# A hybrid decoder block on one core: attention queries and keys turned by VectorE and DMA beside the delta rule, fewer short operations in threshold search and softmax, planner estimates by stage

## The chip, the core and the metric

The kernel runs on one core of a Trainium2 chip. TensorE (PE; PEld is its weight load) multiplies matrices into PSUM, VectorE (DVE), ScalarE (ACT) and GpSimd (POOL) work on SBUF and all but POOL on PSUM, and SyncE (SP) issues nearly all DMAs, one after the other in a fixed order. The metric is the device time of one execution in microseconds. Before the change it is 1774.93 us, the median of three runs from 1773.57 to 1776.5 us.

## The reference, cut to what matters

The input x has 1024 tokens of width 1024. One RMS-normed projection feeds two branches: a gated delta rule with 8 heads (chunked, with a triangular solve for each chunk and a state carried from chunk to chunk), and an attention in which an indexer picks 256 keys for each query. Their gated sum goes through an output projection and then a squared-ReLU MLP of width 4096. What the change touches is the attention branch:

```
a_q = rope(rms_norm(a_q))          # 1024 tokens, 8 heads of 128
a_k = rope(rms_norm(a_k))          # 1024 tokens, 2 heads of 128
score = sum_h w_idx * relu(q_idx . k_idx), causal
_, sel = lax.top_k(score, 256)     # for each query
s = (a_q . a_k[sel]) * 128**-0.5
p = softmax(s);  o = p @ a_v[sel]
```

## The kernel before, in words

All float32 products that matter are made of three single-pass matmuls: each operand is split into a rounded part and a remainder (names `hh` and `hl`, `kTh` and `kTl`, `qh` and `qlo`, ACT makes the first and DVE the second).

The work comes in stages that overlap. First, to about 250 us, the projections of the attention branch: queries and keys are normed, roped and written with tokens as rows to the DRAM tensors `QD` (1024 x 1024) and `KD` (1024 x 256). Then, to about 890 us, the delta rule: for each head PE projects its weights (`dd` matmuls, about 15 us for each group of 128 columns, whose raw weights `w` a DMA brings), and between them, in small float32 matmuls (`tt`, `jj`, `cc`, `oo`), it makes the chunk matrices, joins the inverse and scans the state. Each head's triangular solve runs on POOL, with DMAs ahead of it and behind it (`ZA`, `ZU`). Keys, values and outputs of a head are turned from rows to columns by DVE in 32 x 32 blocks and a DMA that puts the blocks in their places (`by_tokens`, L988, and `output`, L1302, by way of the DRAM tensors `TD` and `TO`).

Beside the delta rule runs the search of the indexer's threshold (`search`, L721): bit by bit from the 32nd down, it counts the scores that reach a candidate. One instance handles the query blocks 2 to 5 with four counts on DVE, one each handles the blocks 6 and 7 with a count on ACT (a sum of signs over 896 and 1024 columns). After each count it does three short DVE operations on one or four columns: `cand<-thr` sets the next bit, `tki<-cnt` judges the count, `thr<-thr,tki` keeps the bit. `select` (L784) then writes the masks.

The attention (about 895 to 1160 us) has 16 steps, one for each block of 128 queries and group of 4 heads (`ATT`). `loadq` (L1422) brings the 128 x 512 queries of a step from `QD` into `ql`. In `score` (L1479) PE turns them by four transposes (`s<-ident,ql`) into one of the two PSUM buffers `s`, ACT and DVE split that into `qh` and `qlo`, and PE multiplies with the keys, up to 512 keys at a time, into the same ring of two buffers. `kprep` (L1390) makes `kTh` and `kTl` in the same way ahead of the first step (`tt<-ident,w`, 16 transposes). `reduce` (L1516) takes each block of scores from PSUM: one DVE operation adds the mask, scales and takes the maximum; for the last block of a row a short one (`nm<-mx`) merges the maxima and changes the sign; ACT takes the exponential with that as bias, and DVE or ACT divides by the sum. `values_out` (L1545) turns the probabilities (`pt<-ident,pr`) and multiplies them with the values (`o`). The output projection (`dd<-hh,m`) fills in between. The MLP follows, to the end.

The order on each engine is fixed when the program is built: the class `Weave` (L2321) lets all these generators run against an estimate of time, takes the ready one of highest priority, and chains the instructions of each engine in that order. Its estimates are the constants of `call` (L2434 to L2459): for instance 0.417 ns for a column of a single-pass matmul, 0.07 us and one element in 1/960 us for DVE, at least 0.5 us for a DMA's issue, and 2.5 us (`SY_LATENCY`) until it has landed. Since every operation is recorded in `call`, all rows of the profile have its line, L2435, and are told apart by their tiles.

Of the kernel before, what the change touches and what calls it, by code (L numbers as in the profile page):

```python
# [20 lines left out]
P = 128  # L21
# [29 lines left out]
def body(tc, a, out, dbg=None):  # L51
# [98 lines left out]
    KD = dr.tile([S, 2 * P], F32, name="KD")  # L150
    GC = dr.tile([H, S], F32, name="GC")
# [467 lines left out]
    scores = {qb: mkp.tile([P, (qb + 1) * P], F32, name=f"sc{qb}") for qb in range(2, NB)}  # L619
# [101 lines left out]
    def search(cs, act):  # L721
        if act is None:
            V_.memset(cand, 0.0)
        yield ("scores", 5 if act is None else act)
        for bit in range(31, -1, -1):
            if bit < 31:
# [3 lines left out]
            if act is None:  # L730
# [5 lines left out]
                lim, cmp = float(TOPK), OP.is_ge  # L736
            else:
                yield "A"
                n = (act + 1) * P
                junk = scp.tile([P, S], F16, name="tkcm")  # L740
                A_.activation(junk[:, :n], scores[act], AF.Sign, scale=-1.0, bias=cand[:, cs],
                              accum_out=cnt[:, cs])
                lim, cmp = float(n - 2 * TOPK), OP.is_le
            yield
            if bit == 31:
                V_.tensor_scalar(thr[:, cs].bitcast(I32), cnt[:, cs], lim, -1.0, op0=cmp, op1=OP.add)
# [6 lines left out]
        if act is None:  # L753
            wv.done("search", 0)
            return


# [78 lines left out]
    for c in ((slice(0, 4), None), (slice(4, 5), 6), (slice(5, 6), 7)):  # L836
        wv.add(8, search(*c))
# [310 lines left out]

    def join(h):
# [203 lines left out]

    wv.add(1, gweights())
    wv.add(9, gdense())
    for u in (6, 5):
        wv.run(until=("put", u))
# [13 lines left out]
    wv.run(until=("masks",))  # L1371
    for c in "kv":
        wv.run(until=("turned", c, H - 1))
# [16 lines left out]
    def kprep():  # L1390
        yield ("out", H - 2)
        for half in range(2):
            t = slot(1, [P, 4, 256], F32)
            SY_.dma_start(t, KD.rearrange("(b p) c -> p b c", p=P)[:, half * 4:half * 4 + 4, :])
            hs = slice(half * HALF, (half + 1) * HALF)
            yield
            for g in range(2):
                yield tt.ready
                ps, slot_ = tt.get()
                for i in range(4):  # L1400
                    PE_.transpose(ps[:, i, :], t[:, i, g * P:(g + 1) * P], ident)
                yield
                pf = ps.rearrange("p a b -> p (a b)")
                A_.activation(kTh[g][:, hs], pf, AF.Copy)
                yield
                V_.tensor_tensor(kTl[g][:, hs], pf, kTh[g][:, hs].bitcast(F32), op=OP.subtract)
                tt.free(slot_)
# [14 lines left out]
    def loadq():  # L1422
        for idx, (qb, g) in enumerate(ATT):
# [3 lines left out]
            SY_.dma_start(ql, QD[qb * P:(qb + 1) * P, g * HALF:(g + 1) * HALF].rearrange("p (h d) -> p h d", h=4))  # L1427
# [51 lines left out]
    def score():  # L1479
        npr = 0  # L1480
        for idx, (qb, g) in enumerate(ATT):
            n = (qb + 1) * P
            yield ("ql", idx)
            yield ss.ready
            ps, slot_ = ss.get()
            ps = ps.rearrange("p (a b) -> p a b", a=4)
            for i in range(4):
                PE_.transpose(ps[:, i, :], lds["q", idx][:, i, :], ident)
# [1016 lines left out]
```

## Time and profile before

| | us |
|---|---|
| median of three runs | 1774.93 |
| the profiled execution | 1774.56 |
| its span, first to last instruction | 1772.8 |
| PE busy in the span | 1754.5 |
| DVE, ACT and POOL busy | 1306.0, 1017.4, 535.8 |

The profiled execution took 1.8 us more than its span (what lies around the program) and 0.4 us less than the median. [...] Matmuls are pipelined, so a row's duration (390 ns for 512 columns) is longer than the step from one start to the next (about 227 ns), and the price of an operation on PE is read from starts.

### The profile page before, as it was taken

How to read it: one execution, taken by the hardware profiler on the slowest of the kernel's cores; microseconds unless marked ns; L12 is line 12 of the kernel's file. 1: busy time of each engine (PE TensorE's matmuls, PEld its weight loads, DVE VectorE, ACT ScalarE, POOL GpSimd, SP SyncE). 2: the span in 40 equal slices, each digit the busy share in tenths (PEclk: the TensorE clock that was granted, in tenths of full speed). 3: DMA queues.
4: the chain of work that ended last, by engine and by line, in shares of the span. 5: the costliest groups of instructions: out<-in, count | busy, mean ns of one | idle time of the engine just before them, and what ended most of it. 6: DMA issues, size and time to landing. Idle time of an engine off the chain costs nothing.

```text
span 1772.8 us, 27516 instructions
## 1 busy us (share of the span) xinstructions
PE 1754.5 (99%) x9657; PEld 1466.5 (83%) x9657; DVE 1306.0 (74%) x2804; ACT 1017.4 (57%) x2074; POOL 535.8 (30%) x772
## 2 busy tenths in 40 slices
PE   9999999999999999999999999999999999999999
PEld 7987998888878888878877888888888888888887
DVE  6557759868788989896467776887666668969673
ACT  7555756666677564554456666676666663333331
POOL 0006430643362441734023121223233232222230
PEclk9999999999999999999999999999999999999999
DMA  5201244444455364445465221325544459373341
GB/s 166 84 13 48 72 129 108 96 121 108 103 134 110 78 144 105 104 110 124 136 222 161 74 81 54 119 84 173 172 161 137 158 198 369 118 251 118 95 138 52
DMA packets 316012, 222.86 MB, mean 126 GB/s; under 512 B 141193, under 2 KB 260194, under 8 KB 315874
## 3 DMA queue, kind: packets, MB, share of 16 engines
q1 hardware_dynamic: 315858, 221.10, 42.8%
q8 instruction: 76, 1.25, 0.3%
q14 instruction: 62, 0.51, 0.1%
q10 hardware_dynamic: 16, 0.00, 0.0%
HBM read 153.23 MB, written 67.83 MB: 125 GB/s over the span
## 4 chain that ended last, share of the span: by engine, by line
PE 89%; DVE 3%; DMA 3%; ACT 2%; SPq 1%; issue 1%; POOL 1%; POOLq 0%; ACTq 0%; DVEq 0%
PE dd L2435 52%; PE o L2435 16%; PE s L2435 7%; PE pt L2435 6%; PE cc L2435 2%; PE sq L2435 2%; PE tt L2435 2%; SPq L2435 1%; PE oo L2435 1%; PE jj L2435 1%; DMA vv<-TO 1%; DVE w L2435 1%; DMA m<-in_w_mlp_down_dram 0%; ACT pr L2435 0%; PE tp L2435 0%
## 5 line engine op out<-in xcount | busy, mean ns | idle before, releaser
L2435 PE MATMUL dd<-hh,w 128*128 128x512 f32 x1552 | 509.3, 401 | 0.0
L2435 PEld LDWEIGHTS dd<-hh,w 128*128 128x128 f32 x1552 | 286.2, 188 | 54.0 <-issue 2.1
L2435 PE MATMUL dd<-hl,w 128*128 128x512 f32 x776 | 310.8, 401 | 0.0
L2435 ACT ACTIVATE m<-m 128x512 fp32r<-128x512 f32 (+1 forms) x240 | 139.8, 625 | 79.1 <-PE o L2435 29.1
L2435 PE MATMUL dd<-hh,m 128*128 128x512 f32 x520 | 172.7, 396 | 0.9 <-ACT ph L2435 0.7
L2435 DVE TENSOR_TENSOR m<-m,m 128x512 fp32r<-128x512 f32 (+2 forms) x184 | 141.1, 794 | 38.7 <-ACT m L2435 33.5
L2435 PEld LDWEIGHTS dd<-hl,w 128*128 128x128 f32 x776 | 146.2, 188 | 26.5 <-issue 0.4
L2435 PE MATMUL dd<-w,hh 128*128 128x256 f32 (+1 forms) x704 | 164.7, 324 | 0.0
L2435 POOL TENSOR_TENSOR stmp<-sx,um 128x60 f32<-128x60 f32 (+24 forms) x186 | 86.4, 465 | 175.1 <-DMA um<-ZA 161.6
L2435 PEld LDWEIGHTS dd<-w,hh 128*128 128x128 f32 x704 | 118.0, 190 | 9.4 <-issue 0.5
L2435 PE MATMUL dd<-w,hl 128*128 128x256 f32 (+1 forms) x352 | 114.2, 324 | 0.0
L2435 PEld LDWEIGHTS dd<-hh,m 128*128 128x128 f32 x520 | 96.4, 188 | 19.2 <-ACT ph L2435 1.1
L2435 POOL TENSOR_TENSOR sx<-sx,stmp 128x60 f32<-128x60 f32 (+24 forms) x248 | 105.3, 425 | 19.4
L2435 DVE TENSOR_SCALAR_CACHE_REDUCE tkeq<-sc,cand 128x384 f16<-128x384 f32 (+3 forms) x128 | 103.0, 805 | 1.1
L2435 PE MATMUL dd<-hl,m 128*128 128x512 f32 x260 | 102.4, 394 | 0.0
L2435 POOL TENSOR_TENSOR m<-m,m 128x512 f32<-128x512 f32 x48 | 69.6, 1459 | 105.7 <-DVE m L2435 58.7
L2435 ACT ACTIVATE hh<-m 128x1024 fp32r<-128x1024 f32 x44 | 45.2, 1056 | 90.7 <-PE s L2435 42.0
L2435 ACT ACTIVATE ha<-m 128x1024 fp32r<-128x1024 f32 x44 | 45.3, 1056 | 86.0 <-PE o L2435 35.1
L2435 DVE TENSOR_TENSOR w<-w,w 128x1024 fp32r<-128x1024 f32 (+1 forms) x63 | 69.3, 1101 | 24.5 <-ACT w L2435 24.3
L2435 ACT ACTIVATE tkcm<-sc,cand 128x896 f16<-128x896 f32 x64 | 69.6, 1088 | 21.1 <-DVE cand L2435 18.8
L2435 PE MATMUL o<-hh,m 128*128 128x512 f32 x248 | 79.6, 389 | 0.0
L2435 PEld LDWEIGHTS dd<-w,hl 128*128 128x128 f32 x352 | 67.0, 190 | 4.5
(433 smaller groups left out, 4358.5 us busy)
## 6 DMA issues: line engine op xcount, KB each, us to landing
HD<-m SPq DMA_DIRECT2D x112, 256.0 KB
m<-HD SPq DMA_DIRECT2D x56, 512.0 KB
w<-in_w_in_dram SPq DMA_DIRECT2D x48, 512.0 KB
m<-in_w_mlp_up_dram SPq DMA_DIRECT2D x33, 512.0 KB
m<-in_w_mlp_down_dram SPq DMA_DIRECT2D x16, 512.0 KB
w<-in_x_dram SPq DMA_DIRECT2D x10, 512.0 KB
wraw<-in_w_in_dram SPq DMA_DIRECT2D x4, 1024.0 KB
es<-GC SPq DMA_DIRECT2D x8, 512.0 KB
```

What stands on the lines that cost most here:

```text
L2435: ins = f(*args, **kw)
```

## The change

1. A new generator `turn_attention` starts when the first head has been scanned. In 20 items (4 for the keys, 16 for the queries) it loads 256 KB from `KD` or `QD` into `ti`, DVE turns it in 32 x 32 blocks into `to`, and four DMAs put the blocks in their places in the new DRAM tensors `KT` and `QT`, in rows of 128 bytes. `ti` and `to` have one buffer each. The delta rule's buffers are not given back before the last item is done.
2. `kprep` loads turned keys from `KT`, and `loadq` turned queries from `QT` (rows of 512 bytes). The 16 + 64 transposes on PE go, and with them the use of `tt` and of one buffer `s` in each step; ACT and DVE split from SBUF. A buffer `ql` is now free when `qlo` is made, before it was when PE had turned it.
3. `search` takes the blocks 6 and 7 together in one instance, with two counts over 1024 columns, and has two short operations for each bit instead of three. What follows it (the next larger score) is its own generator, `above`.
4. `reduce` takes a minimum of negated scores, the second block starting from the first one's result, so that `nm<-mx` goes; the exponential has the scale -1. The second block now waits in the plan for the first.
5. `Weave` gets estimates for each of four stages (`g` from the start of the delta rule's plan, which is also the first to be run, `a`, `u`, `m`), each a few per cent from the constants.

```
+    def turn_attention():
+        yield ("scan", 0)
+        todo = [("k", b) for b in range(0, NB, 2)] + [(g, qb) for qb in (0, 7, 1, 6, 2, 3, 5, 4) for g in range(2)]
+        for w, b in todo:
+            ti = gq.tile([P, HALF], F32, name="ti", bufs=1)
...
+                SY_.dma_start(ti, QD[b * P:(b + 1) * P, w * HALF:(w + 1) * HALF])
...
+            to = gq.tile([P, HALF], F32, name="to", bufs=1)
+            V_.transpose(to, ti)
+            yield
...
+            for r in range(4):
+                SY_.dma_start(dst[r], to[32 * r:32 * r + 32].rearrange("p (y j) -> p y j", j=32))
...
+    wv.add(8, turn_attention())
...
+    wv.run(until=("at", 1, 4))
...
     def score():
-            yield ss.ready
-            ps, slot_ = ss.get()
-            ps = ps.rearrange("p (a b) -> p a b", a=4)
-            for i in range(4):
-                PE_.transpose(ps[:, i, :], lds["q", idx][:, i, :], ident)
-            yield
-            wv.done("qt", idx)
-            A_.activation(qh, ps, AF.Copy)
-            V_.tensor_tensor(qlo, ps, qh.bitcast(F32), op=OP.subtract)
-            ss.free(slot_)
+            A_.activation(qh, ql, AF.Copy)
+            V_.tensor_tensor(qlo, ql, qh.bitcast(F32), op=OP.subtract)
+            wv.done("qt", idx)
...
     def search(cs, acts):
-                V_.tensor_scalar(cand[:, cs].bitcast(I32), thr[:, cs].bitcast(I32), 1 << bit, None,
-                                 op0=OP.bitwise_xor)
...
-                V_.tensor_scalar(tmp[:, cs], cnt[:, cs], lim, float(1 << bit), op0=cmp, op1=OP.mult)
-                V_.tensor_tensor(thr[:, cs].bitcast(I32), thr[:, cs].bitcast(I32), tmp[:, cs],
-                                 op=OP.bitwise_xor)
+                V_.tensor_scalar(ti, cnt[:, cs], lim, float(1 << bit), op0=fail, op1=OP.mult)
+                    V_.scalar_tensor_tensor(ci, ci, 1 << (bit - 1), ti, op0=OP.bitwise_xor, op1=OP.bitwise_xor)
...
     def reduce(idx, i, c, slot_, s_, pi, mx, c0, c1, end):
+        if c:
+            yield ("reduced", idx, i)
-                                op1=OP.max, scale=P ** -0.5, scalar=LOW, accum_out=mx[:, c:c + 1])
+                                op1=OP.min, scale=-P ** -0.5, scalar=mx[:, 0:1] if c else BIG, accum_out=mx[:, c:c + 1])
-        V_.tensor_scalar(nm[:, 0:1], mx[:, 0:1], mx[:, 1:2] if n > HALF else mx[:, 0:1], -1.0,
-                         op0=OP.max, op1=OP.mult)
-        A_.activation(pi[:, :n], pi[:, :n], AF.Exp, bias=nm[:, 0:1], accum_out=nm[:, 1:2])
+        A_.activation(pi[:, :n], pi[:, :n], AF.Exp, scale=-1.0, bias=mx[:, c:c + 1], accum_out=nm[:, 1:2])
...
+COST = {"r": 0.417, "r0": 2.5, "r1": 13.4, "t": 0.835, "f": 1.67, "plat": 0.25, "a0": 0.13, "a1": 1200.0, "alat": 0.15, "v0": 0.07, "v1": 960.0, "vlat": 0.12, "g0": 0.33, "g1": 476.0, "glat": 0.2, "h0": 0.15, "h1": 1000.0}
+    "g": {"r": 0.42154, "r0": 2.58177, "r1": 13.04952, "t": 0.79565, "f": 1.69341, "plat": 0.26166, "a0": 0.13207, "a1": 1204.29497, "alat": 0.14185, "v0": 0.07153, "v1": 964.03542, "vlat": 0.12543, "g0": 0.33522, "g1": 486.29032, "glat": 0.19848, "h0": 0.16299, "h1": 995.55153},
...
```

In the two programs PE's 8720 matmuls become 8640, DVE's 2670 instructions 2472 and SP's 762 DMAs 862; ACT has 1791 in both. PE's order agrees for the first hundred instructions and again in the last 2570, which are most of the MLP; in between it is planned anew everywhere.

How the orders stand against each other at three places. The first is PE between the scores of step 2 (group 0 of query block 7) and of step 3 (group 1); `s<-ident,ql` are the transposes of the queries, `dd` the output projection's or a gate's matmuls. Before:

```order
L2435 MATMUL s<-kTh_9705,qh 128x512
L2435 MATMUL s<-kTl_9707,qh 128x512
L2435 MATMUL s<-kTh_9705,qlo 128x512
L2435 MATMUL s<-ident,ql 128x128 x4
L2435 MATMUL s<-kTh_9706,qh 128x512
L2435 MATMUL s<-kTl_9708,qh 128x512
```

and after:

```order
L2475 MATMUL s<-kTl_9702,qh 128x512
L2475 MATMUL s<-kTh_9700,qlo 128x512
L2475 MATMUL dd<-hh_105,w_10070 128x512
L2475 MATMUL dd<-hh_107,w_10069 128x512
L2475 MATMUL dd<-hl_108,w_10069 128x512
...
L2475 MATMUL dd<-hh_111,w_10070 128x512
L2475 MATMUL s<-kTh_9701,qh 128x512
L2475 MATMUL s<-kTl_9703,qh 128x512
```

Between the two steps stood the four transposes alone; now ten `dd` matmuls stand there, and no transposes. The second place is SP in the delta rule, around the output of the first head (`TO_174` before, `TO_177` after); `w<-in_w_in_dram` are raw weights, `w<-ZA` and `um<-ZU` belong to the triangular solve, `es`, `vv` and `kd` are read by ACT and DVE for the next heads. Before:

```order
L2435 DMA ZA_160<-am 32x8x32 x4
L2435 DMA w_4051<-ZA_160 32x1024 x4
L2435 DMA w_4734<-in_w_in_dram 128x8x128
L2435 DMA QS<-th 1x256 x4
L2435 DMA qss<-QS 128x8x1
L2435 DMA TO_174<-ot 32x32x32 x4
L2435 DMA es<-GC 128x1024
L2435 DMA TDk_187<-cu 32x32x32 x4
L2435 DMA vv<-TO_174 128x8x128
L2435 DMA w_4932<-in_w_in_dram 128x8x128
```

and after:

```order
L2475 DMA ZA_163<-am 32x8x32 x4
L2475 DMA KT<-to 32x16x32 x4
L2475 DMA w_3994<-ZA_163 32x1024 x4
L2475 DMA w_4678<-in_w_in_dram 128x8x128
L2475 DMA ti<-KD 128x2x256
L2475 DMA TO_177<-ot 32x32x32 x4
L2475 DMA QS<-th 1x256 x4
L2475 DMA KT<-to 32x16x32 x4
L2475 DMA vv<-TO_177 128x8x128
L2475 DMA es<-GC 128x1024
L2475 DMA qss<-QS 128x8x1
L2475 DMA w_4859<-in_w_in_dram 128x8x128
```

The stores of `to`, which wait for DVE, stand ahead of the solve's loads and of the raw weights. The third place is DVE in the first step of the attention (`ISA pr,mx<-s,mk` is the operation with the mask, `ISA mx` reads its maximum or minimum). Before:

```order
L2435 TENSOR_TENSOR qlo<-s,qh 128x512
L2435 TENSOR_SCALAR th<-th 128x512
L2435 ISA pr,mx<-s,mk 128x128
L2435 ISA mx 128x1
L2435 ISA pr,mx<-s,mk 128x128
L2435 ISA mx 128x1
L2435 TENSOR_SCALAR nm<-mx 128x1 x2
L2435 ISA pr,mx<-s,mk 128x128
L2435 ISA mx 128x1
L2435 RECIPROCAL mx<-nm 128x1
```

and after:

```order
L2475 TENSOR_TENSOR qlo<-ql,qh 128x512
L2475 ISA pr,mx<-s,mk 128x128
L2475 ISA mx 128x1
L2475 TENSOR_SCALAR th<-th 128x512
L2475 ISA pr,mx<-s,mk 128x128
L2475 ISA mx 128x1
L2475 RECIPROCAL nm<-nm 128x1
L2475 ISA pr,mx<-s,mk 128x128
L2475 ISA mx 128x1
L2475 TENSOR_SCALAR pr<-pr,nm 128x128
```

The split of the queries reads SBUF in place of PSUM, and the short operation `nm<-mx` between the two ISA operations of a row and its exponential is gone.

## Rows read from the trace of the kernel before

**Rows 1.** The page's first part: the span, and each engine's busy time, share of the span and instructions.

```profile
span 1772.8 us, 27516 instructions
PE 1754.5 (99%) x9657; PEld 1466.5 (83%) x9657; DVE 1306.0 (74%) x2804; ACT 1017.4 (57%) x2074; POOL 535.8 (30%) x772
```

**Rows 2.** Busy time of each engine by stage: the projections of the attention branch, the delta rule in three stretches, the attention, the MLP. Columns: stretch, its length, busy us (instructions) of PE, PEld, DVE, ACT and POOL, granted clock, DMA share, GB/s.

```profile
0.00:160.00 160.00, 152.93 (x909) 132.87 (x910) 95.02 (x197) 102.18 (x208) 20.36 (x29) 1.00 0.27 86
160.00:430.00 270.00, 270.00 (x1594) 231.10 (x1592) 208.23 (x571) 169.84 (x388) 108.51 (x208) 1.00 0.39 98
430.00:640.00 210.00, 209.20 (x1448) 173.26 (x1448) 179.59 (x527) 133.74 (x318) 86.25 (x201) 1.00 0.50 112
640.00:900.00 260.00, 258.50 (x1641) 213.48 (x1640) 190.30 (x427) 122.92 (x306) 96.56 (x204) 1.00 0.51 121
900.00:1160.00 260.00, 254.87 (x1360) 211.92 (x1359) 199.08 (x567) 175.20 (x355) 63.72 (x47) 1.00 0.36 114
1160.00:1772.80 612.80, 608.98 (x2713) 503.83 (x2711) 433.79 (x520) 313.56 (x504) 160.42 (x85) 1.00 0.47 160
```

**Rows 3.** The chain of work that ended last, shares of the span by engine.

```profile
PE 89%; DVE 3%; DMA 3%; ACT 2%; SPq 1%; issue 1%; POOL 1%; POOLq 0%; ACTq 0%; DVEq 0%
```

**Rows 4.** The timeline of PE around the first four transposes of queries. Columns: start, us, engine, line, operation, tiles, forms, count.

```profile
895.43 0.62 PE L2435 MATMUL dd<-hh,w 128*128 128x512 f32 x2
895.89 0.60 PE L2435 MATMUL s<-ident,ql 128*128 128x128 f32 x4
896.25 0.48 PE L2435 MATMUL dd<-hl,w 128*128 128x512 f32 x1
896.56 0.63 PE L2435 MATMUL dd<-hh,w 128*128 128x512 f32 x2
```

**Rows 5.** The two groups of transposes that the change removes, by form (the second from the stretch 843 to 900 us): busy us, mean ns of one, idle time before.

```profile
L2435 PE MATMUL s<-ident,ql 128*128 128x128 f32 x64 | 9.6, 273 | 0.1
L2435 PE MATMUL tt<-ident,w 128*128 128x128 f32 x16 | 2.4, 272 | 0.0
```

**Rows 6.** The timelines of PE and of ACT between the scores of step 2 and step 3 (in brackets the idle time before, and who ended it).

```profile
920.25 0.66 PE L2435 MATMUL s<-ident,ql 128*128 128x128 f32 x4
922.36 0.50 PE L2435 MATMUL s<-kTh,qh 128*128 128x512 f32 x1 [1.44 <-ACT qh L2435]
...
920.69 1.14 ACT L2435 ACTIVATE pr<-pr,mx 128x1024 f32<-128x1024 f32 x1
921.73 0.58 ACT L2435 ACTIVATE qh<-s 128x512 fp32r<-128x512 f32 x1
```

**Rows 7.** Who made PE wait in the attention, 900 to 1160 us: total us, times, longest.

```profile
PE s L2435 <- ACT qh L2435: 1.4, 1, 1.4
PE o L2435 <- DVE pl L2435: 1.2, 1, 1.2
```

**Rows 8.** Groups of DVE instructions by form: busy us, mean ns of one, idle time before.

```profile
L2435 DVE TENSOR_SCALAR nm<-mx 128x1 f32<-128x1 f32 x64 | 12.7, 206 | 0.3
L2435 DVE STREAM_TRANSPOSE cu<-t 128x512 f32<-128x512 f32 x16 | 11.2, 702 | 0.1
L2435 DVE TENSOR_TENSOR thr<-thr,tki 128x1 int32<-128x1 int32 x62 | 10.4, 168 | 0.5
L2435 DVE TENSOR_SCALAR tki<-cnt 128x1 int32<-128x1 f32 x64 | 9.4, 146 | 24.2 <-ACT tkcm L2435 24.1
L2435 DVE TENSOR_SCALAR cand<-thr 128x1 int32<-128x1 int32 x62 | 8.9, 143 | 0.0
```

**Rows 9.** Four stores of a head's output in 128-byte rows: their issue on SP, and what the DMA engines did from 567 to 572.3 us, with next to nothing else under way (packets by size; then the queue's packets, MB and share of 16 engines).

```profile
567.10 2.68 SPq L2435 DMA_DIRECT2D TO<-ot  x4
...
DMA packets 4161, 0.53 MB, mean 101 GB/s; under 512 B 4160, under 2 KB 4160, under 8 KB 4160
...
q1 hardware_dynamic: 4160, 0.52, 67.2%
```

**Rows 10.** Pieces of the chain of work in order of time from 654 us on (start, us, what), the matmul that it reaches in PE's timeline, and the sums of such waits: DVE for loads of `vv`, and PE in the stretch 430 to 900 us.

```profile
654.52 2.79 SPq L2435
...
659.57 4.71 DMA vv<-TO
...
664.30 0.44 DVE vv L2435
...
666.20 0.27 DVE sst L2435
...
666.52 0.49 PE L2435 MATMUL cc<-sst,kt 128*128 128x128 f32 x2 [0.67 <-DVE sst L2435]
...
DVE vv L2435 <- DMA vv<-TO: 11.9, 5, 4.2
...
PE cc L2435 <- DVE sst L2435: 1.3, 2, 0.7
PE cc L2435 <- ACT svn L2435: 1.0, 2, 0.8
```

**Rows 11.** A load of raw weights, the shortest time from its issue on SP to its split on ACT in the stretch 430 to 900 us, and a load of 512 KB in the chain.

```profile
445.05 0.70 SPq L2435 DMA_DIRECT2D w<-in_w_in_dram  x1
...
450.60 1.06 ACT L2435 ACTIVATE w<-w 128x1024 fp32r<-128x1024 f32 x1 [0.68 <-PE dd L2435]
...
512.39 5.92 DMA es<-GC
```

More of the change, by code (lines that the diff above doesn't have):

```diff
@@ L150, in body @@
     KD = dr.tile([S, 2 * P], F32, name="KD")
+    QT = [dr.tile([NB * 4 * P, P], F32, name=f"QT{g}") for g in range(2)]
+    KT_ = dr.tile([NB * 2 * P, P], F32, name="KT")
     GC = dr.tile([H, S], F32, name="GC")
@@ L616, in misc_post @@
         SY_.dma_start(GC.rearrange("h (b p) -> (h b) p", p=P), gr)
-    scores = {qb: mkp.tile([P, (qb + 1) * P], F32, name=f"sc{qb}") for qb in range(2, NB)}
+    full = {qb: mkp.tile([P, S if qb > 5 else (qb + 1) * P], F32, name=f"sc{qb}") for qb in range(2, NB)}
+    scores = {qb: t[:, :(qb + 1) * P] for qb, t in full.items()}
     def iq_post(u, out):
@@ L1391, in kprep @@
         yield ("out", H - 2)
[L1392 to L1395, printed above, removed]
+        for g in range(2):
+            t = slot(1, [P, S], F32)
+            SY_.dma_start(t.rearrange("p (b t) -> p b t", t=P), KT_.rearrange("(b g d) t -> g d b t", g=2, d=P)[g])
             yield
-            for g in range(2):
-                yield tt.ready
-                ps, slot_ = tt.get()
-                for i in range(4):
-                    PE_.transpose(ps[:, i, :], t[:, i, g * P:(g + 1) * P], ident)
+            for half in range(2):
+                hs = slice(half * HALF, (half + 1) * HALF)
+                A_.activation(kTh[g][:, hs], t[:, hs], AF.Copy)
                 yield
-                pf = ps.rearrange("p a b -> p (a b)")
-                A_.activation(kTh[g][:, hs], pf, AF.Copy)
+                V_.tensor_tensor(kTl[g][:, hs], t[:, hs], kTh[g][:, hs].bitcast(F32), op=OP.subtract)
                 yield
-                V_.tensor_tensor(kTl[g][:, hs], pf, kTh[g][:, hs].bitcast(F32), op=OP.subtract)
-                tt.free(slot_)
         wv.done("K")
@@ L1766, in body @@
     EARLIER = sorted(qb for qb, g in ATT[:-1] if not g and qb // 4 != first and qb != ATT[-1][0])
+    wv.estimates("a")
     wv.add(1, kprep())
@@ L1802, in body @@
     wv.run(until=("pv", NA - 2))
+    wv.estimates("u")
     wv.add(8, norm2())
@@ L2301, in body @@
     pA_es.close()
+    wv.estimates("m")
     mp, mp_es = pool("mp", side="right")
@@ L2327, in __init__, with estimates @@
         self.busy, self.last, self.ev, self.chains = {}, {}, {}, []
-        self.shared, self.port = False, []
+        self.shared, self.port, self.cost = False, [], dict(COST)
+    def estimates(self, stage):
+        self.cost = {**COST, **STAGES.get(stage, {})}
     def engine(self, eng, name):
@@ L2432, in __getattr__ @@
         name, wv = self.name, self.wv
+        c = wv.cost
         def call(*args, **kw):
```

89 lines of the change are left out of this document (58 added, 31 removed), and 3 rows, old and new, of the table STAGES.

## The prediction

> **What bounds the kernel now.** I read the page's first part, then the stages, then the chain of work, then the timelines at the places that the change touches.
>
> PE is busy for 1754.5 of 1772.8 us [rows 1], and the chain that ended last is PE for 89% [rows 3]. The stages say where the other 18.3 us lie: PE is idle for 7.1 us before 160 us, 0 to 430 us, 0.8 and 1.5 us in the delta rule, 5.1 us in the attention and 3.8 us in the last stage, nearly all of that behind the last matmul [rows 2]. DVE, the next engine, reaches 86% at most, in the stretch 430 to 640 us (179.59 of 210 us). So time is won here in two ways only: fewer steps on PE, or fewer of the few gaps. What ACT, DVE, POOL or the DMAs gain or lose counts only where it makes or closes a gap on PE.
>
> **The change, part by part.**
>
> *The transposes leave PE.* Their price is read from starts. Two ordinary matmuls ahead of the first group start at 895.43 and the transposes at 895.89, so one matmul is a step of 0.23 us. From the transposes' start to the second matmul behind them (896.56) it is 0.67 us, of which one matmul takes 0.23; four transposes cost 0.44 us [rows 4]. Some of that is that the first matmul behind them takes longer (0.31 in place of 0.23 us). There are 16 such groups in the attention and 4 in `kprep`: 20 x 0.44 = 8.8 us. The other price is the groups' busy time, 9.6 + 2.4 = 12.0 us [rows 5], but it counts the overlapping tails of pipelined matmuls; 8.8 is the step and I take it. In the attention and the end of the delta rule there is always a `dd` matmul to follow, so all of it falls off the end.
>
> [...]
>
> *The wait that goes with them.* Between steps 2 and 3 PE turns the queries and then has nothing else in its order until `qh` is made: ACT is in a 1.14 us scaling of probabilities from 920.69, makes `qh` from 921.73, and PE stands still for 1.44 us [rows 6], the longest of its waits in the attention [rows 7]. In the new order no PE result stands between the load and `qh`, and ten `dd` matmuls lie between the scores of the two steps. The wait goes: -1.4 us. What is late next is `pl` on DVE (1.2 us, once) [rows 7].
>
> *Softmax.* 64 operations `nm<-mx` of 206 ns go, 13.2 us of DVE's 199 in the attention [rows 8, 2], and each stood between a row's scores and its exponential. They are off PE's path except through waits like that for `pl`; DVE's load falls from 77% to 72%. Bounds: 0, and the rest of the attention's 5.1 us, 3.7. I take 1 us, since only the `pl` wait is named by a row as DVE's. The second block's wait for the first is within DVE, which does them in this order anyway, at about nothing; it would cost only if a block's PSUM buffer came free later, by one 0.7 us operation.
>
> *Search.* Before, 3 instances x 31 bits x 3 short operations; after, 2 x 31 x 2: 155 fewer at about 150 ns [rows 8], -23 us of DVE beside the delta rule. The 20 new block transposes take 20 x 0.70 = 14 us of it [rows 8]. Net -9 us in about 400, on no path: 0. The wider sign count of block 6 is 32 x 0.1 us on ACT, which is idle for a third of that stretch and more [rows 2]: 0.
>
> *The new DMAs.* Each item issues a load and four stores. Such stores take SP 0.67 us each (2.68 for four), and the 16 engines were 67.2% busy over 5.3 us, 3.6 us, for their 4096 packets [rows 9]. The new ones have half as many packets: 1.8 us of all engines and 2.7 us of SP's queue for each item, 36 and 54 us in all, within some 300 us in which the DMA engines are half busy [rows 2]. The plan counts 0.5 us for an issue. What this can do is in the chain at 654 us: SP is in stores for 2.79 us, the load of `vv` lands 4.71 us after its issue, DVE, which works in order, stands before its product, `sst` comes late, and PE waits 0.67 us [rows 10]. Five such waits of DVE, 11.9 us together, and all of PE's waits in the delta rule are 2.3 us [rows 10]; that is about 0.2 us of PE for 1 us of DVE. Bounds: below, 0, if the plan puts the stores where nobody is waiting; below nothing it can't be, since DMAs are only added there. Above: each of the 20 items holds up one such load by its 2.7 us, 54 x 0.2 = 10.8 us. Most loads have some slack, as 5 waits on 7 loads averaged 2.4 us and PE felt few of them; I take +1.5.
>
> *The queries' loads* come in 512-byte rows into two buffers that are held a little longer, until `qlo`. A buffer's next load has a whole step's time (about 16 us, 260 / 16 [rows 2]), a load of twice the size lands in 5.92 us [rows 11]: 0; it would cost up to a step's wait of 1.4 us if that cover went.
>
> *The estimates* move instructions from the first hundred on, but the last 2570 matmuls keep their order. What they can touch are the gaps: at best most of the 7.1 us in the projections, at worst gaps of the same size again. No row speaks for a sign; I take 0 and keep -4 and +5.
>
> **The sum.** Against the profiled execution, 1774.56 us: -8.8 - 1.4 - 1.0 + 1.5 = -9.7, so 1764.9; the median of the runs is 0.4 us above that execution. I forecast 1765 us.
>
> **The rivals.**
>
> *The queue eats the gain.* The stores of `to` stand ahead of the solve's and the heads' loads, as the order on SP shows; if most items hold up a load that is waited for, the upper bound above holds: 1765 - 1.5 + 10.8 = 1774, no change. For it: DVE is the fullest engine there, and the stores wait for it, so SP stands too. Against: DVE gets 9 us lighter, and PE lost only 2.3 us in 470 to all waits so far. Chance 0.14. [...]
>
> *Weights come late* (the other side). PE's `dd` matmuls cover every other wait; if their weights are late, nothing does. The shortest time from a load's issue to its split is 5.55 us (445.05 to 450.60), and 512 KB takes up to 5.92 us to land [rows 11], so that load has no slack. A store ahead that waits for DVE holds SP; it decides from the point where the load's slack, some 5 us in most cases, is gone. If each of the 20 items then delays PE by 1 us, it is 1765 + 20 = 1785, slower. Against it: no wait of PE for `w` is among its waits in the delta rule [rows 10]. Chance 0.08.
>
> *The gaps close too.* With the shorter chain in the attention and another order in the projections, 6 to 8 of the 12.2 us of gaps go beside the transposes: about 1757. For it: all but one of the attention's waits end with ACT or DVE, which both get freer. Against: a lighter PE also needs its operands sooner. Chance 0.15.
>
> **How the numbers follow.** The forecast, 1760 to 1770, has 0.63. What a measurement can tell from no change is about 0.2%, 3.5 us: faster is below 1771.4, slower above 1778.5. Forecast and closing gaps are faster, and of the queue's rival, which spreads from 1770 to 1778, about 0.04: 0.82. The rest of that rival is the same, 0.10. The weights are slower, 0.08. The range from 1755 to 1773 leaves out the weights, half of the queue's rival and the far end of the gaps.
>
> **What would show it.** The rows `s<-ident,ql` and `tt<-ident,w` gone and PE's busy time 9 to 12 us lower (1743 to 1746); no wait of PE for `qh`; PE's idle time within 3 us of 18.3; DVE's busy time some 20 us lower. For the queue's rival, DVE and ACT would wait more than 30 us for `vv`, `kd` and `es`, and PE more than 6 us for `cc` operands; for the weights', rows of PE or ACT waiting for `w`. I am wrong if PE's idle time in the delta rule or the attention grows by more than 6 us, or if its busy time falls by less than 8.

## The result, and the profile after

The changed kernel takes 1763.69 us (median of six runs, 1763.16 to 1764.46), the kernel before, on the same chip, 1775.33 us (1773.57 to 1776.5): ratio 0.9935, 95% interval 0.9923 to 0.9948. That is 11.6 us less, 0.65%, and 1.3 us under the predicted 1765.

The page's first part for the changed kernel answers to [rows 1]:

```profile
span 1762.7 us, 27331 instructions
PE 1745.7 (99%) x9577; PEld 1462.3 (83%) x9577; DVE 1306.2 (74%) x2606; ACT 1020.2 (58%) x2074; POOL 554.2 (31%) x773
```

PE is busy for 8.8 us less and idle for 17.0 us in place of 18.3; DVE is as busy as before. The same stretches as in [rows 2]:

```profile
0.00:160.00 160.00, 153.12 (x904) 133.16 (x905) 94.03 (x190) 101.25 (x207) 20.48 (x30) 1.00 0.26 86
160.00:430.00 270.00, 270.00 (x1632) 231.66 (x1633) 205.55 (x485) 168.44 (x381) 111.53 (x206) 1.00 0.38 99
430.00:640.00 210.00, 209.25 (x1429) 172.90 (x1420) 181.66 (x472) 140.97 (x332) 91.75 (x203) 1.00 0.66 147
640.00:900.00 260.00, 260.00 (x1648) 216.37 (x1647) 199.43 (x454) 125.67 (x313) 102.46 (x205) 1.00 0.56 136
900.00:1160.00 260.00, 256.92 (x1345) 214.88 (x1344) 201.54 (x506) 181.56 (x364) 71.02 (x52) 1.00 0.35 112
1160.00:1762.70 602.70, 596.40 (x2646) 493.30 (x2644) 424.03 (x502) 302.35 (x480) 156.92 (x79) 1.00 0.47 162
```

PE's idle time in the delta rule (third and fourth row) is 0.75 us where it was 2.3, in the attention 3.1 where it was 5.1. The last stretch has 6.3 us where it had 3.8. So something was gained ahead of 1160 us and some of it lost behind.

What was lost stands in the MLP. PE's list of waits begins with one that the kernel before doesn't have, and no wait for `qh` is left in it (compare [rows 7]):

```profile
PE o L2475 <- ACT m L2475: 2.5, 1, 2.5
PE dd L2475 <- DVE w L2475: 1.7, 2, 1.1
PE tp L2475 <- DVE iqs L2475: 1.7, 2, 1.3
```

That wait in PE's timeline, and ACT's ahead of it:

```profile
1218.33 0.39 PE L2475 MATMUL o<-hh,m 128*128 128x512 f32 x1
1221.23 4.61 PE L2475 MATMUL o<-w,m 128*128 128x512 f32 x12 [2.51 <-ACT m L2475]
```

```profile
1216.26 1.71 ACT L2475 ACTIVATE m<-m,vecs 128x256 f32<-128x256 f32 x4 [2.31 <-DMA m<-in_w_mlp_up_dram]
1220.58 0.60 ACT L2475 ACTIVATE m<-o 128x512 f32<-128x512 f32 x1 [2.61 <-issue]
```

PE waits 2.51 us for an operation of ACT. Then the same twelve matmuls that take 2.88 us in the kernel before take 4.61. The windows of 5 us around it say why (the third number from the right is the granted clock):

```profile
1215.00:1220.00 5.00, 3.72 (x17) 2.75 (x15) 3.35 (x4) 1.71 (x4) 3.85 (x2) 1.00 1.02 347
1220.00:1225.00 5.00, 3.77 (x10) 2.94 (x11) 3.13 (x4) 3.23 (x7) 2.50 (x2) 0.66 0.26 100
1225.00:1230.00 5.00, 5.00 (x24) 4.13 (x23) 4.92 (x8) 2.03 (x4) 0.03 (x1) 0.99 0.23 87
```

In the middle row the mean is 0.66. In windows of 0.5 us the granted clock reads 1.00 up to 1221.5 us, 0.65 in the next, 0.50 from 1222 to 1225 us, 0.94 in the next and 1.00 after it; half of some 3.4 us at 0.50 is the 1.7 us by which the twelve matmuls are longer. Wait and slow matmuls together cost 2.51 + 4.61 - 2.88 = 4.2 us. PE's last 2560 matmuls, which keep their order, begin at 1188.25 us in the kernel before and at 1173.79 in this one: 14.5 us were won by then, 4.3 were given back. So the 8.8 us less of PE's busy time are some 10.5 less work and 1.7 more for the clock, and the 1.3 us less of idle time are 3.8 less and 2.5 more.

ACT's timeline puts its 2.61 us down to "issue". The trace's semaphore records say more: ACT stands at a semaphore until 1220.54 us, and the last part of the second of six stores `HD<-m` (256 KB each, SP's second line below), issued at 1213.70, lands at 1220.51.

```profile
1211.93 1.00 SPq L2475 DMA_DIRECT2D m<-in_w_mlp_up_dram  x2
1213.02 5.11 SPq L2475 DMA_DIRECT2D HD<-m  x6
```

It lands 6.8 us after its issue, where the median of the 112 such stores is 2.3 and the plan counts 2.5: two loads of 512 KB went out just ahead of it, and the DMA engines are full (a share of 1.02 from 1215 us). In the kernel before SP issues these two loads after the 16th store of the MLP, in the change after the 14th. The fourteen programs of this document fall in two lots: the seven with 14 have this wait of PE (1.2 to 2.5 us), the seven with 16 don't.

### The profile page after: what moved, and what is told of

It is laid out like the page before. It is cut to its first block, busy times and chain, and to the rows that moved or that the text cites. A ratio compares the mean times of both kernels' runs of the same rounds, so it can differ in the third digit from the quotient of the medians.

```text
span 1762.7 us, 27331 instructions
## 1 busy us (share of the span) xinstructions
PE 1745.7 (99%) x9577; PEld 1462.3 (83%) x9577; DVE 1306.2 (74%) x2606; ACT 1020.2 (58%) x2074; POOL 554.2 (31%) x773
## 4 chain that ended last, share of the span: by engine, by line
PE 91%; DVE 4%; ACT 2%; issue 1%; DMA 1%; SPq 1%; POOL 0%; DVEq 0%; ACTq 0%; POOLq 0%
PE dd L2475 54%; PE o L2475 15%; PE s L2475 7%; PE pt L2475 6%; PE cc L2475 2%; PE sq L2475 2%; PE tt L2475 2%; PE oo L2475 1%; SPq L2475 1%; DVE m L2475 1%; PE jj L2475 1%; DVE w L2475 1%; DVE pr L2475 0%; DMA irl<-in_x_dram 0%; PE tp L2475 0%
## 5 line engine op out<-in xcount | busy, mean ns | idle before, releaser
L2475 ACT ACTIVATE m<-m 128x512 f32<-128x512 f32 (+1 forms) x240 | 140.4, 625 | 95.9 <-PE dd L2475 39.2
L2475 DVE TENSOR_TENSOR m<-m,m 128x512 fp32r<-128x512 f32 (+2 forms) x184 | 149.1, 832 | 43.1 <-ACT m L2475 37.3
L2475 PEld LDWEIGHTS dd<-hl,w 128*128 128x128 f32 x776 | 146.2, 188 | 27.5 <-issue 1.2
L2475 POOL TENSOR_TENSOR sx<-sx,stmp 128x60 f32<-128x60 f32 (+24 forms) x248 | 117.5, 474 | 19.4
L2475 POOL TENSOR_TENSOR m<-m,m 128x512 f32<-128x512 f32 x48 | 65.8, 1383 | 99.5 <-DVE m L2475 54.7
L2475 ACT ACTIVATE ha<-m 128x1024 fp32r<-128x1024 f32 x44 | 45.2, 1056 | 88.2 <-PE s L2475 40.8
L2475 DVE TENSOR_TENSOR w<-w,w 128x1024 fp32r<-128x1024 f32 (+1 forms) x63 | 70.3, 1116 | 21.0 <-ACT w L2475 18.7
L2475 ACT ACTIVATE tkcm<-sc,cand 128x1024 f16<-128x1024 f32 x64 | 73.1, 1142 | 0.8 <-ACT tkcm L2475 0.4
L2475 ACT ACTIVATE w<-w 128x1024 fp32r<-128x1024 f32 x48 | 50.7, 1055 | 37.9 <-PE dd L2475 36.2
```

Of the source, the lines that this page charges most:

```text
L2475: ins = f(*args, **kw)
```

## The experiments

Except where a plan is said to be made anew, an edit is hidden from the plan, so that all other instructions stand in the same order on each engine; the start of each matmul can then be compared with that of its twin, and a difference that grows shows the place of a cost. "Against the changed kernel" is the difference of the two ratios times 1775 us; the two intervals together leave some 3 us either way, so that +0.9, +0.5 and -2.0 tell nothing and +3.7 little.

Two things blur what the end shows. In place, executions differ without any edit: after_pe_back, after_nm_back and after_no_um are the change up to 890 us, yet PE loses 0.5, 0.5 and 1.8 us on its twins between 160 and 885 us. And a program that keeps the change's order and comes later into the MLP gets back a part of the 4.2 us lost there, for the larger part because the clock stays up: 2.7 us in after_pe_back, 1.8 in after_nm_back, 2.9 and 2.5 in after_stores_twice and after_stores_small, all four with a granted clock of 1.00 in the windows of 5 us from 1205 to 1240 us, and 0.2 in after_search_back, where it is 0.83 from 1220 to 1230 us. So the cost in place is given beside the cost at the end.

| kernel | median us | ratio to before, 95% interval | against the changed kernel | span, PE busy, PE idle (us, profiled) |
|---|---|---|---|---|
| the change | 1763.69 | 0.9935 [0.9923, 0.9948] | | 1762.7, 1745.7, 17.0 |
| after_pe_back | 1769.32 | 0.9964 [0.9952, 0.9977] | +5.1 | 1768.5, 1752.1, 16.4 |
| after_nm_back | 1768.26 | 0.9964 [0.9951, 0.9978] | +5.1 | 1766.3, 1747.3, 19.0 |
| after_nm_planned | 1779.92 | 1.0028 [1.0017, 1.0038] | +16.5 | 1778.9, 1750.8, 28.1 |
| after_search_back | 1766.37 | 0.9956 [0.9943, 0.9968] | +3.7 | 1764.8, 1746.1, 18.7 |
| after_stores_twice | 1773.17 | 0.9997 [0.9987, 1.0006] | +11.0 | 1770.4, 1747.6, 22.8 |
| after_stores_small | 1764.49 | 0.9940 [0.9928, 0.9953] | +0.9 | 1762.8, 1744.1, 18.7 |
| after_flat | 1774.13 | 0.9990 [0.9981, 0.9999] | +9.8 | 1772.2, 1749.2, 23.0 |
| after_no_um | 1762.45 | 0.9924 [0.9912, 0.9936] | -2.0 | 1761.3, 1745.2, 16.1 |
| after_g_only | 1764.31 | 0.9938 [0.9926, 0.9951] | +0.5 | 1762.3, 1744.8, 17.5 |
| before_est | 1792.29 | 1.0091 [1.0077, 1.0105] | | 1790.3, 1762.8, 27.5 |
| before_unturned | 1771.61 | 0.9983 [0.9974, 0.9992] | | 1773.5, 1752.2, 21.3 |
| before_unturned_planned | 1775.33 | 1.0003 [0.9994, 1.0012] | | 1772.5, 1750.4, 22.1 |

**The transposes.** after_pe_back puts the queries' 16 groups of four back on PE; their results are not used.

```
                     s_, slot_ = ss.get()
+                    if i == 0 and c == 0:
+                        for j in range(4):
+                            wv.issue("PE", PE.transpose(s_[:, j * P:(j + 1) * P], ql[:, j, :], ident), 0.0, 0.0)
```

> The changed kernel with the 64 transposes of queries put back on PE, into the PSUM buffer that the step's first scores then overwrite; nothing reads them, and the plan does not count them, so that every other instruction keeps its place. Theory (the gain is PE's steps): 16 groups at 0.44 us, +7.0 us over the changed kernel's 1763.7, so 1770.7 (1769.5 to 1772), with PE's idle time as it was. Rival (the gain is the new plan's, and transposes lie beside other work): within 2 us of 1763.7.

PE's timeline around one of these groups reads like [rows 4]:

```profile
964.62 0.39 PE L2478 MATMUL dd<-hl,m 128*128 128x512 f32 x1
964.85 0.60 PE L1533 MATMUL s<-ident,ql 128*128 128x128 f32 x4
965.20 0.48 PE L2478 MATMUL s<-kTh,qh 128*128 128x512 f32 x1
965.52 0.40 PE L2478 MATMUL s<-kTl,qh 128*128 128x512 f32 x1
```

From 964.85 to 965.52 it is 0.67 us, of which one matmul's step is 0.23: 0.44 us again. Against their twins the matmuls behind a group start 0.44 to 0.46 us later, at each of the 16 places, 7.2 us together; by 1215 us PE is 8.4 us behind, 0.9 of it from ahead of the first group. Then the wait in the MLP is 1.3 us in place of 2.5, the granted clock stays at 1.00, and 2.7 us come back. The price of a group is right, and what the end sees is 5.1 us (5.8 by the profiled spans).

before_unturned takes the same 16 groups out of the kernel before, in its order (`qh` and `qlo` are made from unturned queries, so the attention's numbers are others); before_unturned_planned lets the plan know of it.

```
-                PE_.transpose(ps[:, i, :], lds["q", idx][:, i, :], ident)
+                wv.phantom("PE", (P * 0.835 + 2.5) / 1e3, 0.25)
...
+            ps = lds["q", idx]
```

> The kernel before, whose order of all other instructions stays as it is, without the 64 transposes of the queries on PE (16 groups of four); qh and ql are made from the unturned queries, so the output is not the reference's. Theory of the prediction: 16 x 0.44 = 7.0 us and the 1.4 us wait for qh go, 1775.3 - 8.4 = 1767. Rival, by the price that the transposes showed when they were put back into the changed kernel (5.6 us): 1769.7 with the wait left, 1768.3 without. Second rival, the transposes filled gaps that stay open: within 2 us of 1775.

> The kernel before without the 64 transposes of the queries on PE, as before_unturned (qh and ql from the unturned queries, the output not the reference's), but the plan no longer counts them, so the attention is ordered anew with the old constants. Behind the plan's back the ratio was 0.9983, 3 us, where 8.4 were expected. Theory, the order that still kept their place left waits open, and a new one closes them: 0.9945 to 0.9965, 1765.5 to 1769. Rival, with the old constants the attention's new order is no better, since the changed kernel with them also had 5.6 us more of idle time there: 0.9975 to 1.0, 1771 to 1775.

Neither came near its theory: -3.0 us and nothing (0.9983 and 1.0003). In before_unturned 14 of the 16 removed groups bring 0.43 to 0.45 us at their places, 6.2 us together; the other two bring nothing, since right behind them PE waits anyway, for `qh` and for `pl`. In the profiled execution two waits lead PE's list:

```profile
PE cc L2441 <- DVE sst L2441: 2.7, 1, 2.7
PE s L2441 <- ACT qh L2441: 2.2, 1, 2.2
```

The granted clock is down to 0.77 around the end of the first. Behind the second, which ends at 925.31 us, it stays at 1.00; it falls to 0.66 behind a shorter wait, of 1.22 us for `pl`:

```profile
720.00:725.00 5.00, 2.34 (x9) 1.86 (x8) 4.96 (x8) 0.79 (x4) 4.61 (x6) 0.77 0.69 212
...
925.00:930.00 5.00, 4.69 (x22) 3.60 (x23) 4.75 (x13) 5.00 (x9) 2.23 (x2) 1.00 0.52 154
...
974.95 0.55 PE L2441 MATMUL o<-pl,vh 128*128 128x512 f32 x1 [1.22 <-DVE pl L2441]
...
975.00:980.00 5.00, 5.00 (x18) 4.08 (x19) 2.81 (x8) 0.67 (x3) 1.28 (x1) 0.66 0.49 152
```

The wait for `qh` did not go with the transposes but grew from 1.4 to 2.2 us: ACT, whose order is kept, makes `qh` at 924.64 us, behind two scalings of 1.14 us. The wait for `sst` (2.66 us, up to 722.95 us) stands ahead of the edit, where the order is that of the kernel before, which waits 0.67 us there; it hangs on a load of `vv`, and eleven runs of this kernel spread from 1768.8 to 1775.7 us. The profiled one took 1775.29, and PE was 3.5 us behind its twins ahead of the first removed group. Made anew with the old constants, the plan gave back in the attention's last part what it had won: PE's matmuls were 5.4 us ahead of their twins at 1140 us and level from 1180. At 1140 us three waits follow each other, of 0.49, 0.70 and 1.20 us, and the granted clock is 0.83 over these 10 us:

```profile
1144.21 0.47 PE L2441 MATMUL s<-ident,w 128*128 128x128 f32 x1 [1.20 <-DVE w L2441]
...
1140.00:1150.00 10.00, 7.60 (x31) 5.82 (x30) 8.60 (x15) 6.72 (x16) 2.62 (x2) 0.83 0.73 218
```

**The estimates.**

```
-        self.cost = {**COST, **STAGES.get(stage, {})}
+        self.cost = dict(COST)                                                    # after_flat
+        self.cost = {**COST, **(STAGES[stage] if stage in "ga" else {})}          # after_no_um
+        self.cost = {**COST, **(STAGES[stage] if stage == "g" else {})}           # after_g_only
```

before_est is the kernel before with `STAGES` and the four calls of `estimates`, nothing else.

> The changed kernel with the constants of before in every stage of the plan. Theory (PE's steps; the estimates have no sign of their own): 1763.7 within 4 us either way. Rival (the estimates carry the gain): 1769 or more.

> The changed kernel with its estimates g and a, and the constants of before in the stages u and m. In the changed kernel PE's last 2560 matmuls take 4.3 us more than the same ones before, nearly all of it around a wait of 2.5 us at 1218 us for ACT. Theory: the order that ACT, DVE and SP got from the estimates u and m makes this wait; without them it is gone, 1759.5 (1758 to 1761). Rival: the wait comes with the state in which the MLP is entered, whatever the estimates there: 1763 to 1765, with a wait of 2 us or more at the same place.

> The kernel before with the estimates by stage alone. Theory (PE's steps): 1775.3 within 4 us either way. Rival (the estimates carry the gain): 1769 or less.

> The changed kernel with the estimates of the first stage (projections and delta rule) alone; from the attention on the old constants. With no estimates the ratio was 0.999, with those of the first two stages 0.9924. By the traces the kernel without estimates had 2.2 us more in changes between float32 and single-pass matmuls before 160 us and 5.6 us more of PE's idle time in the stretch from 900 to 1150 us. Theory, the two parts add: 0.9965 to 0.998, 1769 to 1771. Rival, the estimates of the attention alone matter: 0.9985 to 0.9995. Second rival, those of the first stage alone: 0.992 to 0.9935.

Without estimates nearly the whole gain is gone (0.999), the rival's case; put into the kernel before they make it 16 us slower, which neither expectation had. The first stage's alone come out where all four do (0.9938), next to the second rival's range. Without those of the last two the MLP's long wait is not there, as the theory had it, and SP issues the two loads after the 16th store; but the time, 1762.45, is not the theory's 1758 to 1761. PE comes into the MLP 3.2 us behind its twins, 1.8 of them from the delta rule, where the two programs are the same, and wins 4.7 there; the 2.0 us at the end lie within the intervals. The attention, 900 to 1150 us, by the windows of the change, of after_flat and of after_g_only, in this order:

```profile
900.00:1150.00 250.00, 246.92 (x1298) 206.69 (x1297) 191.54 (x493) 175.53 (x351) 66.37 (x49) 1.00 0.36 114
```

```profile
900.00:1150.00 250.00, 241.35 (x1250) 197.81 (x1249) 187.68 (x491) 169.30 (x343) 62.36 (x45) 0.99 0.38 121
```

```profile
900.00:1150.00 250.00, 245.46 (x1283) 203.88 (x1282) 191.33 (x488) 172.77 (x345) 64.92 (x48) 1.00 0.35 114
```

PE is idle for 3.1, 8.7 and 4.5 us. So 5.6 of after_flat's 9.8 us are gaps in the attention, among them waits of 1.9 us for `qh` and three for `pl` (2.2 us together), with the clock at 0.83 from 920 to 930 us. Yet after_g_only orders its attention by the same old constants and hasn't them. So the constants of the attention alone do not make these gaps; what the plan is like when it comes out of the first stage has a part, and how, is not settled. No other set of constants was run, so how far orders spread is known from these few alone. The ends hide a part of it, too. Into the MLP PE comes 13.6 us behind the change in after_flat and 4.2 in after_g_only, and both win 4.7 there, where SP issues the two loads after the 16th store. That the first stage's estimates alone end level with all four is therefore in part chance. One reading in the expectation of after_g_only fell: it put 2.2 us down to changes between float32 and single-pass matmuls before 160 us, but at 250 us the matmuls of after_flat are level with those of the change (0.2 us ahead). before_est has the largest gaps, one of 2.95 us in the attention and one of 2.2 us at 205 us, with a granted clock of 0.70 from 935 to 940 us and of 0.75 from 205 to 210 us.

**Softmax.** after_nm_back puts a short DVE operation ahead of each of the 64 exponentials; in after_nm_planned the plan counts it.

```
+        nn = pA.tile([P, 2], F32, name="nn", bufs=8)
+        wv.issue("V", V.tensor_scalar(nn[:, 0:1], mx[:, c:c + 1], 1.0, None, op0=OP.mult), 0.0, 0.0)
-        A_.activation(pi[:, :n], pi[:, :n], AF.Exp, scale=-1.0, bias=mx[:, c:c + 1], accum_out=nm[:, 1:2])
+        A_.activation(pi[:, :n], pi[:, :n], AF.Exp, scale=-1.0, bias=nn[:, 0:1], accum_out=nm[:, 1:2])
```

> The changed kernel with a short VectorE operation (the row's maximum times 1.0 into a tile of its own) put back ahead of each of the 64 exponentials, the order otherwise the same. Theory of the prediction: +1.0 us, 1764.7, between 0 and 3.7. Rival, DVE has room in the attention: within 0.5 us of 1763.7 with DVE's busy time 8 to 13 us higher.

> The changed kernel with the same 64 short VectorE operations ahead of the exponentials as in after_nm_back, but here the plan counts them, and so orders the attention with them (342 VectorE and 183 ACT instructions from the attention on stand elsewhere). Put in behind the plan's back they cost 0.29% (ratio 0.9964 against 0.9935), some 5 us. Theory, what costs is the work that the order doesn't know, and the plan can hide 13 us of VectorE in the attention: 0.9930 to 0.9945, 1763 to 1766. Rival, the longer way from a row's scores to its exponential costs this in any order: 0.9958 to 0.997. Second rival, any new order of the attention falls out by luck, by more than either: outside both.

Behind the plan's back it costs 5.1 us by the ratios and 3.6 by the profiled spans, where the bound was 3.7. The place is mostly the first fifth of the attention: PE is 0.8 us behind its twins at 895 us, where no operation has been added yet, 2.2 at 908, 2.5 at 930, 4.3 at 949 and still at 1056 us, and 5.4 at 1145. That is 4.6 us in place, of which the MLP gives back 1.8. PE's waits in that first fifth, where the change has none:

```profile
904.36 0.50 PE L2479 MATMUL o<-pl,vh 128*128 128x512 f32 x1 [0.34 <-DVE nn L1558]
906.15 0.33 PE L2479 MATMUL pt<-ident,pr 128*128 128x128 f32 x1 [0.26 <-ACT pr L2479]
...
943.83 0.39 PE L2479 MATMUL s<-kTh,qh 128*128 128x256 f32 x1 [0.46 <-DVE mx L2479]
```

With the plan told of the operations it is 1.0028, 16.5 us over the change, the second rival's case. PE is idle for 14.2 of 250 us in the attention. Its longest wait there, at the end, has no `dd` matmul between `o` and the next transposes, and the clock's mean over the 10 us around it is 0.67; the windows and PE's timeline:

```profile
900.00:1150.00 250.00, 235.85 (x1228) 194.77 (x1227) 189.68 (x535) 161.24 (x318) 59.30 (x43) 0.99 0.34 110
1140.00:1150.00 10.00, 5.54 (x22) 4.24 (x22) 8.37 (x14) 4.18 (x9) 2.80 (x2) 0.67 0.58 186
```

```profile
1144.52 0.99 PE L2478 MATMUL s<-ident,w 128*128 128x128 f32 x2 [2.82 <-DVE w L2478]
```

**Search.**

```
+            if bit < 31:
+                tj = scp.tile([P, 6], I32, name="tkj")
+                for _ in range(3 if first_ else 2):
+                    wv.issue("V", V.tensor_scalar(tj[:, cs], cnt[:, cs], lim, 1.0, op0=ok, op1=OP.mult), 0.0, 0.0)
```

> The changed kernel with 155 short VectorE operations of six columns put back into the bits of the search, the order otherwise the same. Theory of the prediction: on no path, 0 us, 1763.7 within 1 us, with DVE's busy time 11 to 23 us higher. Rival, DVE is the fullest engine in the delta rule and each us of it costs PE 0.2 us: +2 to +5 us, 1766 to 1769.

DVE's busy time rises by 26.1 us (1332.3), more than either expected, and 3.7 us are lost by the ratios, 2.1 by the spans. In place it is 2.9 us between 160 and 885 us, among them 0.5 us at 392, 0.7 around 457 and 1.1 around 535, where PE now waits 0.86 us for `sr` of DVE. That is the rival's case, though not far outside the spread of unedited stretches. And the edit puts back more than the change took out: the 155 operations take 35 us, while the short operations of the search took 47.7 us before and take 27.6 in the change.

**The stores.** after_stores_twice issues each of the 80 stores of `to` once more into a spare tensor; after_stores_small does so with one row of 2 KB for each, in place of 64 KB in rows of 128 bytes.

```
                 SY_.dma_start(dst[r], to[32 * r:32 * r + 32].rearrange("p (y j) -> p y j", j=32))
+                wv.issue("SY", SY.dma_start(dst2[r], to[32 * r:32 * r + 32].rearrange("p (y j) -> p y j", j=32)), 0.0, 0.0)
```

> The changed kernel with every store of the turned tile issued twice, the second time into a spare tensor: 80 more stores on SP's queue, about 0.5 us of SP each (40 us in all), and again as many small packets; the order of all other instructions is the same. Theory of the prediction (0.2 us of PE for each us that DVE waits): between 0 and +10.8 us, the value taken for the first 80 was +1.5, so 1765.2. Rival, the queue matters: over +6 us, 1770 and more. Second rival, the queue has room for them: within 0.7 us of 1763.7, and DVE's waits for the loads of vv under 5 us in all.

> The changed kernel with 80 more stores on SP's queue as in after_stores_twice, but each of a single row of 2 KB into consecutive addresses of the spare tensor in place of 512 packets of 128 bytes; the order of all other instructions is the same. after_stores_twice cost 0.62% (ratio 0.9997 against 0.9935), 11 us. Theory, what delays the loads is the time that SP's queue spends on an issue and the waits of the DMA engines behind the small packets together; with the packets gone less than half is left: ratio under 0.996. Rival, the number of issues is what costs: over 0.998, near 0.9997. Second rival, the packets alone: 0.993 to 0.9942.

Twice the stores cost 11.0 us by the ratios and 7.7 by the profiled spans, the same number of small ones 0.9 and 0.1. The ends flatter the small ones: in place, from 160 to 885 us, they cost 3.1 us and the large ones 10.1, and the MLP gives back 2.5 and 2.9. Three of the places are the same in both (near 515, 563 and 745 us). So the larger part is what the DMA engines have to move, and the issues on SP's queue cost up to a third of it; the theory's and the second rival's ranges overlap at 0.9940 and are not told apart. The waits of DVE and ACT for loads in the delta rule, first in the change, then in after_stores_twice (total us, times, longest):

```profile
DVE vv L2475 <- DMA vv<-TO: 0.5, 1, 0.5
ACT es L2475 <- DMA es<-GC: 1.1, 1, 1.1
ACT kd L2475 <- DMA kd<-TDk: 0.2, 1, 0.2
```

```profile
DVE vv L2479 <- DMA vv<-TO: 5.1, 4, 3.4
ACT es L2479 <- DMA es<-GC: 10.3, 4, 4.0
ACT kd L2479 <- DMA kd<-TDk: 3.1, 3, 1.6
```

With `to` (1.8 and 8.2 us) and `vv<-TDv` (0.5 and 3.0) the waits grow from 4.1 to 29.7 us (in after_stores_small to 11.7), and PE's 10.1 us in place make 0.4 us of PE for 1 us of waiting (3.1 for 7.6 in after_stores_small, the same rate). DVE stands still at `vv` for 0.5 us where it was 11.9 [rows 10]: the change brought 80 stores and 20 loads more, and fewer such waits.

How much the DMA engines move in their time differs between two stretches: stores in pieces of 128 bytes move 101 GB/s with 67.2% of the engines' time taken [rows 9], an estimated 150 (101 / 0.672) at full use, and from 1215 to 1220 us in the change, where 87 of 1239 packets are under 512 bytes, 347 GB/s go at a share of 1.02. That the size of the pieces makes this difference is not shown: the two runs with more stores don't tell it from the amount, since the 80 rows of 2 KB also moved less, 0.16 in place of 5.2 MB.

## Why the prediction was right, and where it wasn't

The bound held: PE's steps and gaps made the time. The sum of -9.7 us came near what was measured, -11.6 by the medians and -10.1 between the two profiled executions, but several of its terms were off and made up for each other. That it came so near is in part luck: with the old constants the same change has 23.0 us of idle time on PE where the kernel before has 18.3, and brings 1.8 us; with the new estimates it has 17.0. The forecast needed the gaps to stay, and no row could tell that they would.

- *Transposes, -8.8*: the price is right, a group costs 0.43 to 0.46 us at 30 of the 32 places where it was put in or taken out. PE's busy time fell by the same 8.8 us by chance, as the net of 10.5 and the 1.7 of the clock. The step "all of it falls off the end" is what doesn't hold in general: a wait right behind a group takes it back (two places), and of 6.2 us in place 3.0 came off the kernel before, none with a plan made anew.
- *The wait for `qh`, -1.4*: gone, as forecast. The transposes alone did not cause it: taken out of the kernel before, with ACT's order as it was, they left a wait of 2.2 us.
- *Softmax, -1.0, bounds 0 to 3.7*: mis-sized; the undo costs 3.6 to 5.1 us, 4.6 in place. The bound took only gaps that the trace of before has, while in the new order the first steps of the attention have DVE on the way from scores to product.
- *Search, 0*: probably mis-sized; the undo costs 2.1 to 3.7 us, but puts back 35 us of DVE for 20 taken out. "On no path" was wrong by the section's own rate, since a fuller DVE makes `cc` and `tt` operands late in the delta rule.
- *DVE some 20 us lower*: not seen (1306.0 and 1306.2). The 20 block transposes take the 14.0 us forecast, but the products `m<-m,m` of the MLP take 8.0 us more than before (152.2 and 144.2), the masked reduce 2.0 more (55.1 and 53.1), and the busy time counts the overlapping parts of neighbours once: the search's short operations fell by 20 us by their durations, where 23 were forecast, but the time in which DVE does nothing else fell by only 6.8, and by 6.1 for the 13.2 us of `nm<-mx`.
- *New DMAs, +1.5, bounds 0 to 10.8*: the mechanism is real, the rate is 0.4 and not 0.2, and most of it is what the DMA engines move, with SP's issues at up to a third; but for the first 80 stores the plan found places where hardly anybody waits. The lower bound, "below nothing it can't be", was wrong: the waits for `vv`, `kd` and `es` fell from 20.0 to 1.8 us, since the change moves the other instructions too.
- *Estimates, 0, between -4 and +5*: the largest miss. They are worth 9.8 us in the changed program and cost 16 us in the kernel before. "At best most of the gaps in the projections" looked at gaps that exist, and a new order can open others: a plan told of 64 more operations of 0.15 us lost 16.5 us.
- *What no term had*: 4.3 us are given back in the MLP by a new wait and the clock behind it. The new order on SP puts two loads of 512 KB ahead of a store whose landing ACT needs, and the plan's 2.5 us for a landing was 6.8.

Undone one by one, the parts (16 of the 20 groups of transposes, softmax, search, estimates: 5.1 + 5.1 + 3.7 + 9.8 = 23.7 us) cost twice what the change brought, 11.6. They are not shares of a sum. A likely reading, not tested by itself, is that an order that fits one set of durations has little slack for another; but after_nm_planned, whose order knew its operations, did worse still. Of the rivals, the queue that eats the gain didn't happen, though after_stores_twice shows it at twice the stores (0.9997, no change), at the price that it was given. Putting the queries' transposes back on PE costs 5.1 us in this kernel. But no run takes DVE's and the DMAs' part away at the same time, so transposes on PE and those by DVE and DMAs are not priced against each other. The gaps did close in part, by 3.8 us up to the MLP; of late weights there is one wait of ACT, 1.6 us, and none of PE.

after_no_um has the lowest ratio of all (0.9924 [0.9912, 0.9936]); that it is faster than the change is not shown, as the intervals overlap.

## What to carry to other kernels

Where the critical engine is 99% busy, price a removed step by the starts of its neighbours, not by its busy time; that number held to a few hundredths of a microsecond in two programs, except where a wait on another engine stood right behind. Then ask whether the order around it is made anew: in a kernel whose order comes from a plan, the luck of the new order (here from -10 to +16 us) is larger than most edits, belongs into the range, and is measured by changing the estimates alone. To find where a change lands, keep the order, and compare each instruction's start with that of its twin; a wait further on can give back what was lost, so the end alone misleads. And where a wait is put down to nothing, look at the DMAs: here a store behind two large loads landed after 6.8 us where the plan counted 2.5.

## What the runs showed of the hardware

In the change a wait of PE cost more than itself: behind its 2.51 us the granted clock read 0.50 from 1222 to 1225 us, and twelve matmuls took 4.61 in place of 2.88 us, 1.7 us on top. The granted clock was also below 1.00 at waits of 2.95 us (before_est, 0.70 from 935 to 940 us), 2.19 us (before_est, 0.75 from 205 to 210 us), 2.82 us (after_nm_planned, 0.50 from 1145 to 1150 us), 2.66 us (before_unturned, 0.77 from 720 to 725 us), 2.34 us (after_search_back, 0.83 in the two windows of 5 us from 1220 us) and 1.87 us (after_flat, 0.73 from 925 to 930 us), but likewise at 1.22 us (before_unturned, 0.66 from 975 to 980 us) and at 1.20 us with two shorter waits just ahead (before_unturned_planned, 0.83 from 1140 to 1150 us). It was 1.00 behind 2.31 us (after_nm_back, 1220 to 1230 us) and 2.2 us (before_unturned, 925 to 930 us), and in the kernel before, whose waits are 1.44 us at most, in every window of 50 us up to 1750 us. So in these runs the length of the wait alone does not tell the two groups apart; what else does, they don't show.

In the change, six stores behind two large loads landed later than the median store. The median of the 112 stores `HD<-m` of 256 KB is 2.3 us from issue to landing; those six, behind two loads of 512 KB at 1212 us, took 5.2 to 7.0 us.
